# A hybrid decoder layer on one core: key norms as two float32r products of split squares, compressed tokens with 129 columns, pinned orders of pair 4 and of the last pair of a group, and a two-operation scaling

## The chip, the cores and the metric

The kernel is one program on one core of a Trainium2 chip. TensorE (PE) does the matrix products and transposes, VectorE (DVE), ScalarE (ACT) and GpSimd (POOL) the work on elements, and SyncE (SP) and ACT issue most transfers. The metric is the device time of one execution in microseconds (us): lower is better.

## The reference

One decoder layer for 512 tokens of width 1024, in float32. What the change touches, cut from the reference:

```python
kk = heads(k * k_k)                                            # RWKV-7 half, 16 heads of 64
kk = kk / jnp.maximum(jnp.sqrt(jnp.sum(kk * kk, axis=-1, keepdims=True)), 1e-12)
...
cidx = np.arange(n_cmp)[:, None] * CMP_STRIDE + np.arange(CMP_BLOCK)[None, :]   # 31 blocks of 32 tokens, stride 16
def compress(t, pos, w1, w2):                                  # sparse attention half, 4 groups of keys and values
    blk = kv(t)[:, :, cidx] + pos.astype(f32)
    hid = jax.nn.gelu(blk.reshape(B, G, n_cmp, CMP_BLOCK * DH) @ w1.astype(f32))
    return hid @ w2.astype(f32)
...
e = jnp.where(mask, jnp.exp(s - jnp.max(s, axis=axis, keepdims=True)), 0.0)     # masked softmax
return e / jnp.maximum(jnp.sum(e, axis=axis, keepdims=True), TINY)
```

The layer normalises its input, projects it, runs RWKV-7 time mixing (16 heads) and sparse attention (compressed, selected and window branches, 16 heads) beside each other, merges them by gates, and ends with a gated feed-forward block.

## The kernel before, in words

**Products.** A large product with float32 inputs is done as three products of type float32r: each factor is split into a high part (a copy rounded to float32r) and a low part (the rest), and high by high, high by low and low by high are summed. `proj_steps` (L302 to L309) does one block of a projection so: 8 steps, each of three products 128x512 (L306, L307, L308), with a yield after each step. A step is called a group below, a group of three products. Its weights come in two halves; each half is loaded by a transfer that SP issues, copied to the high part by ACT (L124, called from `split_to`), and subtracted to the low part by POOL (L162). Each of these has three buffers, so the copy of a later half waits until PE has finished with an earlier one. Smaller products are left in float32; the trace records a float32 product as two PE instructions.

**Order.** Python generators lay out the work. `inputs` (L493) projects K, R and V of a pair of heads, `prep` (L526) makes decay, gates and key norms of the pair, `couple` (L581) makes the products between keys and queries within chunks of 64 tokens, `invert` (L644) inverts the chunks' triangles on DVE, `recur` (L688) runs the recurrence, and `finish` (L829) closes a group. The eight pairs form two groups of GP = 4: pairs 0 to 3 and 4 to 7. `drive` (L453) steps the projections and gives the other generators a step at fixed rates; a yield marks where one may be left for another. A scheduler then fixes the order of instructions on each engine. Each engine runs its list in that order. `keep_in_program_order` pins an instruction's place among its engine's others.

**Shifts.** A projection's result is mixed with its own shift by one token: `shift_a` on ACT (L333) and `shift_b` on DVE (L336), both reading the projection's bank of PSUM. `shift_b` of K is pinned at step SK = 4 of the projection of R. Two banks (`pj`) are used in turn by the projections of K, R, V and the others.

**Key norms.** `prep` squares the scaled keys (Q, L531, ACT), multiplies them by a matrix of ones (`onesr`, in float32, L548), which sums within each head and spreads the sums over its rows (pb); DVE bounds pb below (L549), ACT takes Ln (L555) and Exp (L556), and DVE uses it in KB (L567) and AR (L570). The gates (pw L533, pa L541) stand ahead of it; POOL's T (L538) lies between pw and the scan (L539). Tiles of the tag "T" (Q, C, T, F, EN and others) share NT = 6 buffers.

**couple.** After two yields PE transposes V (pv, L140) and multiplies KB by AR (g, L605, two banks of `pz` and two of `py`); after more yields it transposes KB (pt) and does pl and pbo.

**invert.** The inversion of a group is a chain of small DVE instructions (TM L660, XP L662), 30 steps, beside which the next projections run. Group 0's chain runs while pair 4's K and R are projected.

**Compression.** `cproj` (L384) projects the tokens to be compressed into KC, with one array of 33 columns for each of four groups and a fifth for the positions; `compress` (L405) multiplies 16 slices of it by w1 in float32 (hid, L412: 155 columns, five times 31), and yields after every fourth.

**Attention.** `score` (L1051) makes the probabilities of a pair of heads; `norm` (L1063) divides them: for each piece of 128 queries and 128 to 512 keys one `tensor_scalar` by a column of reciprocals on DVE and one on POOL (both L1073). The pieces are then transposed on PE (pt, L140).

Of the kernel before, what the change touches and what calls it, by code (L numbers as in the profile page):

```python
# [10 lines left out]
F32 = mybir.dt.float32  # L11
F32R = mybir.dt.float32r
AF = mybir.ActivationFunctionType
OP = mybir.AluOpType
# [28 lines left out]
def hybrid_layer(ctx: ExitStack, tc: tile.TileContext, a, out, dbg=None, stop=None):  # L43
# [33 lines left out]
    def pz(name):  # L77
        return pzs[-1][1].tile([128, 512], F32, tag="pz", name=name, bufs=2)
# [253 lines left out]
    def shift_a(p, o, mc, n=128):  # L332
        sc.activation(o, p[:n], AF.Copy, scale=omm[:n, mc:mc + 1])  # L333
# [50 lines left out]
    def cproj(kv):  # L384
        KC = cp.tile([128, 5, 8, 33], F32, tag="KC", name=f"KC{kv}", bufs=2)
        KCs.append(KC)
        po.memset(KC[:, 4], 0.0)
        pos = cp.tile([64, 32], F32, tag="pos", name=f"pos{kv}", bufs=2)
        sy.dma_start(pos, a["posk" if kv == 0 else "posv"])
        po.memset(KC[:, 0:4, :, 32:33], 0.0)  # L390
        for i in range(2):
            po.tensor_copy(KC[64 * i:64 * i + 64, 4, :, 0:2].rearrange("p r q -> p q r"),
                           pos.rearrange("p (q r two) -> p q r two", r=8, two=2)[:, :, :, i])
        for half in range(2):
# [6 lines left out]
            for e in range(2):  # L401
                for i in range(2):
                    sc.dma_start(KC[64 * i:64 * i + 64, 2 * half + e, :, 0:32], z[e * 64:e * 64 + 64, i])

    def compress(kv):  # L405
# [5 lines left out]
        for l in range(16):  # L411
            te.matmul(ph[:, 0:5 * NCMP], w1[:, l, :], KCs[kv][:, :, l % 8, l // 8:l // 8 + NCMP],  # L412
                      start=l == 0, stop=l == 15)
            if l % 4 == 3:
                yield
        hb = cp.tile([128, 1], F32, tag="hb", name=f"hb{kv}", bufs=2)
        ve.tensor_copy(hb, ph[:, 4 * NCMP:4 * NCMP + 1])
        u = cp.tile([128, 4, 32], F32, tag="hu", name=f"hu{kv}", bufs=2)
        w = cp.tile([128, 4, 32], F32, tag="hv", name=f"hv{kv}", bufs=2)
        po.memset(u, 0.0)  # L420
        ve.tensor_scalar(u[:, :, 0:NCMP], ph[:, 0:4 * NCMP].rearrange("p (g n) -> p g n", n=NCMP), hb, None,
                         op0=OP.add)
# [70 lines left out]
    def inputs(p, o):  # L493
        K = o.K = rw.tile([128, S], F32, tag="K", name=f"K{p}", bufs=2)
        pk = pj(f"k{p}")
        yield from proj_steps(4 + 3 * p, f"k{p}", pk)
        shift_a(pk, K, 8 + p)
        R = o.R = rw.tile([128, S], F32, tag="R", name=f"R{p}", bufs=1)
        pr = pj(f"r{p}")
        for i, _ in enumerate(proj_steps(3 + 3 * p, f"r{p}", pr)):  # L500
            if i == SK:
                tc.keep_in_program_order(shift_b(pk, K, 8 + p))
            yield
# [22 lines left out]
    def prep(p, o, gr=None):  # L526
        K, R, VW, lh, ll = o.K, o.R, o.VW, o.lh, o.ll
        V = VW[:, 64:]
        kkc = vec[:, V_KK + p:V_KK + p + 1]
        Q = rw.tile([128, S], F32, tag="T", name=f"Q{p}", bufs=NT)  # L530
        sc.activation(Q, K, AF.Square, scale=kkc)  # L531
        pw = pz(f"pw{p}")
        te.matmul(pw, lh[:, :128], ltw, start=True, stop=False)  # L533
# [10 lines left out]
        F = rw.tile([128, S], F32, tag="T", name=f"F{p}", bufs=NT)  # L544
        sc.activation(F, pa, AF.Identity, scale=hka[:, p:p + 1], bias=oka[:, p:p + 1])
        yield
        pb = pz(f"pb{p}")
        te.matmul(pb, onesr.bitcast(F32), Q, start=True, stop=True)  # L548
        ve.tensor_scalar(pb, pb, 1e-24, None, op0=OP.max)  # L549
# [31 lines left out]
    def couple(p, o, gr, i):  # L581
# [6 lines left out]
        sc.activation(gr.Dc[:, i], EC[:, :, 64], AF.Copy)  # L588
        yield
        yield  # L590
        for q in range(2):
# [459 lines left out]
    def score(p8, o):  # L1051
# [11 lines left out]
        def norm(e, qb, k):  # L1063
# [7 lines left out]
            for b in range(2):  # L1071
                i = b * 4 + k
                (po if b else ve).tensor_scalar(o.pe[e, b, k], o.pe[e, b, k], st[e][:, 3, i:i + 1], None, op0=OP.mult)  # L1073

# [514 lines left out]
```

## Time and profile before

| | us |
|---|---|
| median of 3 runs | 1169.26 (1168.82 to 1169.72) |
| profiled execution, its own time | 1168.92 |
| its span in the trace | 1167.1 |
| busy: PE | 1145.0 |
| busy: DVE, ACT, POOL | 587.8, 584.0, 580.5 |

The granted TensorE clock has a mean of 0.997. The span runs from the first to the last instruction; 1.8 us of the execution's own time lie outside it. In the rows of the profile "L" is the line in the kernel, then come engine, operation and tile, written from left to right as result and inputs. A row of the timeline begins with start and duration in us; what stands in brackets is how long the engine was idle before it, and what it waited for. Matmuls are pipelined: a product's duration (0.39 us) is longer than the distance to the next one's start, and it is this distance that counts.

### The profile page before, as it was taken

The numbers are of one execution on the slowest core, as the hardware profiler recorded it, in microseconds if no ns is written. First come the engines' busy times: TensorE is split into PE (matmuls) and PEld (weight loads), VectorE is DVE, ScalarE is ACT, GpSimd is POOL, SyncE is SP. The second block draws the span as 40 slices with busy tenths as digits, with TensorE's granted clock in tenths as the row PEclk, the third lists the DMA queues.
The fourth block names the chain that finished last, engine by engine and source line by source line (L and its number), as shares of the span: only waits on it lengthen the run. The fifth ranks groups of instructions, "written<-read, shape, count | busy, mean of one in ns | idle before, by whom it ended". The sixth has DMA issues, their size and how long they took to land.

```text
span 1167.1 us, 19728 instructions
## 1 busy us (share of the span) xinstructions
PE 1145.0 (98%) x7338; PEld 916.2 (79%) x7338; DVE 587.8 (50%) x1194; ACT 584.0 (50%) x1150; POOL 580.5 (50%) x526
## 2 busy tenths in 40 slices
PE   9999999999999999989999999999999999999997
PEld 7888878777887887656677778889888888888886
DVE  4226666534676642677798745754443343331103
ACT  5537664453666434567676654434444444443311
POOL 4335654425655443477766635511565566554440
PEclk9999999999999999999999999999999999999999
DMA  6433235321433664115552136641233333334421
GB/s 235 126 83 80 84 105 166 111 86 44 133 113 103 190 182 128 56 42 149 168 156 89 46 98 182 211 153 37 83 99 99 95 95 100 99 94 134 135 64 72
DMA packets 95507, 131.95 MB, mean 113 GB/s; under 512 B 34033, under 2 KB 36913, under 8 KB 95154
## 3 DMA queue, kind: packets, MB, share of 16 engines
q1 hardware_dynamic: 79490, 116.26, 33.3%
q10 hardware_dynamic: 15920, 14.42, 4.0%
q8 instruction: 58, 0.95, 0.3%
q14 instruction: 39, 0.32, 0.1%
HBM read 108.30 MB, written 19.14 MB: 109 GB/s over the span
## 4 chain that ended last, share of the span: by engine, by line
PE 91%; DVE 4%; ACT 2%; POOL 2%; issue 1%; DVEq 0%; POOLq 0%; ACTq 0%
PE pu L221 6%; PE pu L223 6%; PE pu L222 6%; PE dn L1321 3%; PE dn L1320 3%; PE dn L1319 3%; PE o L1146 3%; PE pt L140 3%; PE ub L1203 3%; PE gt L306 2%; PE ub L1205 2%; PE ub L1204 2%; PE gt L307 2%; PE gt L308 2%; PE v L306 2%; PE v L307 2%
## 5 line engine op out<-in xcount | busy, mean ns | idle before, releaser
L1099 ACT ACTIVATE p<-p,stt 128x384 f32<-128x384 f32 (+3 forms) x128 | 70.7, 554 | 35.1 <-DVE stt L1097 33.4
L1073 POOL TENSOR_SCALAR p<-p,stt 128x512 f32<-128x512 f32 (+1 forms) x64 | 72.9, 1149 | 30.7 <-DVE stt L1068 16.4
L1461 DVE SCALAR_TENSOR_TENSOR u<-pu,cvec,u 128x511 f32<-128x511 f32 x44 | 33.0, 749 | 101.1 <-ACT u L1460 101.1
L1097 DVE CUSTOM_DVE_ANT_0 p<-s,rh 128x384 f32<-128x384 f32 (+3 forms) x128 | 59.2, 485 | 24.6 <-PE s L1083 18.9
L140 PE MATMUL pt<-ident,p 128*128 128x128 f32 x320 | 44.7, 274 | 2.9 <-POOL p L1073 2.0
L1467 DVE TENSOR_TENSOR al<-u,ah 128x512 fp32r<-128x512 f32 x22 | 23.9, 1085 | 45.5 <-ACT ah L1466 45.5
L140 PEld LDWEIGHTS pt<-ident,p 128*128 128x128 f32 x320 | 37.9, 141 | 7.8 <-POOL p L1073 2.5
L1146 PE MATMUL o<-PT,vt 128*64 128x384 f32 (+3 forms) x256 | 43.9, 448 | 0.0
L1465 POOL TENSOR_TENSOR u<-u,u 128x512 f32<-128x512 f32 x22 | 28.4, 1290 | 27.2 <-DVE u L1462 26.3
L1090 PE MATMUL s<-kst,qs 128*128 128x512 f32 (+1 forms) x128 | 38.5, 390 | 2.6 <-DVE stt L1097 2.4
L1460 ACT ACTIVATE u<-pu,cvec 128x512 f32<-128x512 f32 x44 | 33.6, 765 | 3.0 <-PE pu L1423 3.0
L1462 DVE SCALAR_TENSOR_TENSOR u<-pu,cvec,u 128x510 f32<-128x510 f32 x44 | 33.0, 749 | 1.6
L1073 DVE TENSOR_SCALAR p<-p,stt 128x512 f32<-128x512 f32 (+1 forms) x64 | 33.2, 548 | 0.8
L1137 ACT ACTIVATE PT<-pt 128x512 f32<-128x512 f32 x48 | 27.6, 586 | 9.2 <-PE pt L140 8.8
L1146 PEld LDWEIGHTS o<-PT,vt 128*64 128x64 f32 x256 | 16.8, 136 | 19.4 <-issue 17.5
L1090 PEld LDWEIGHTS s<-kst,qs 128*128 128x128 f32 x128 | 21.4, 189 | 10.7 <-DVE stt L1097 6.2
L1367 DVE TENSOR_TENSOR p2ss<-p2ss 128x1 f32<-128x1 f32 x4 | 0.6, 161 | 52.1 <-ACT p2jl L1365 52.1
L1139 DVE COPY PT<-pt 128x512 f32<-128x512 f32 x32 | 21.6, 676 | 8.3 <-PE pt L140 8.3
L1466 ACT ACTIVATE ah<-u 128x512 fp32r<-128x512 f32 x22 | 13.9, 633 | 22.1 <-POOL u L1465 22.1
L1099 ACT ACTIVATION_READ_ACCUMULATOR p<-p,stt 128x1 f32 x128 | 24.1, 189 | 0.0
L809 ACT ACTIVATE UV<-xs 64x256 f32<-64x256 f32 x16 | 6.0, 378 | 35.0 <-PE xs L804 34.6
L662 DVE TENSOR_TENSOR XP<-XP,TM 128x30 f32<-128x30 f32 (+14 forms) x60 | 20.3, 338 | 2.0
(1758 smaller groups left out, 3939.4 us busy)
## 6 DMA issues: line engine op xcount, KB each, us to landing
gtd<-gt ACTq DMA_DIRECT2D x16, 256.0 KB, 2.8
qs<-qd SPq DMA_DIRECT2D x32, 128.0 KB, 3.3
g<-gtd SPq DMA_DIRECT2D x16, 256.0 KB, 3.0
xt<-in_x_dram SPq DMA_DIRECT2D x4, 512.0 KB, 5.2
bvd<-bv SPq DMA_DIRECT2D x8, 256.0 KB, 2.3
bvl<-bvd SPq DMA_DIRECT2D x8, 256.0 KB, 2.9
kst<-kst ACTq DMA_DIRECT2D x16, 128.0 KB, 2.3
t<-oad SPq DMA_DIRECT2D x8, 256.0 KB, 3.3
```

What stands on the lines that cost most here:

```text
L140: return te.transpose(o, i, ident)
L221: te.matmul(p, wh(k), mh(k), start=first and k == 0, stop=False)
L222: te.matmul(p, wh(k), ml(k), start=False, stop=False)
L223: te.matmul(p, wl(k), mh(k), start=False, stop=last and k == n - 1)
L306: te.matmul(p, wh(k), hh[:, k, :], start=k == 0, stop=False)
L307: te.matmul(p, wh(k), hl[:, k, :], start=False, stop=False)
L1073: (po if b else ve).tensor_scalar(o.pe[e, b, k], o.pe[e, b, k], st[e][:, 3, i:i + 1], None, op0=OP.mult)
L1090: m = te.matmul(s_[:, :n], qt, kt[:, x, b, :n], start=x == 0, stop=x == 1)
L1097: ve.tensor_tensor_reduce(sb, parts[b], rh[e][:, (3 - qb) * 128:], -1.0, BIG, OP.add, OP.min, st[e][:, 0, i:i + 1])
L1099: sc.activation(sb, sb, AF.Exp, scale=-1.0, bias=st[e][:, 0, i:i + 1], accum_out=st[e][:, 1, i:i + 1])
L1146: te.matmul(acc[e * 64:e * 64 + 64, j * 128:], vt[:, j, b * 256 + g * 64:b * 256 + g * 64 + 64], m[e][:, c:c + n], start=False, stop=k == ...
L1203: te.matmul(p, wh(k), sh[:, k, :], start=k == 0, stop=False)
```

## The change

1. **Compressed tokens.** KC becomes one array with the position columns first (0 and 1) and the four groups behind them with 32 columns each. A slice for a product is then 129 neighbouring columns instead of five pieces of 31. Four POOL memsets go. The 16 products of a kind stand in two runs of eight instead of four of four.
2. **Key norms.** Q is split into Qh (ACT copy) and Ql (POOL subtraction), and pb is the sum of two float32r products with `onesr`. They are written directly behind the gate products, before the yield. That is 8 more ACT copies, 8 more POOL subtractions, and two more tiles of tag "T" for each pair.
3. **Pair 4.** `shift_b` of its K is written directly behind `shift_a`, and no longer pinned at step 4 of R.
4. **couple.** The last pair of each group (3 and 7) yields three times, not twice, ahead of the transposes and the products g.
5. **Scaling.** POOL's `tensor_scalar` in `norm` gets a second operation, a multiplication by 1.0; the one on DVE stays.

```diff
--- before.py
+++ after.py
@@ -382,14 +382,12 @@
     KCs = []
 
     def cproj(kv):
-        KC = cp.tile([128, 5, 8, 33], F32, tag="KC", name=f"KC{kv}", bufs=2)
+        KC = cp.tile([128, 8, 130], F32, tag="KC", name=f"KC{kv}", bufs=2)
         KCs.append(KC)
-        po.memset(KC[:, 4], 0.0)
         pos = cp.tile([64, 32], F32, tag="pos", name=f"pos{kv}", bufs=2)
         sy.dma_start(pos, a["posk" if kv == 0 else "posv"])
-        po.memset(KC[:, 0:4, :, 32:33], 0.0)
         for i in range(2):
-            po.tensor_copy(KC[64 * i:64 * i + 64, 4, :, 0:2].rearrange("p r q -> p q r"),
+            po.tensor_copy(KC[64 * i:64 * i + 64, :, 0:2].rearrange("p r q -> p q r"),
                            pos.rearrange("p (q r two) -> p q r two", r=8, two=2)[:, :, :, i])
         for half in range(2):
             p = pj(f"kc{kv}{half}")
@@ -400,7 +398,8 @@
                 sc.activation(z[:, i], pv[:, i], AF.Copy)
             for e in range(2):
                 for i in range(2):
-                    sc.dma_start(KC[64 * i:64 * i + 64, 2 * half + e, :, 0:32], z[e * 64:e * 64 + 64, i])
+                    c = 2 + 32 * (2 * half + e)
+                    sc.dma_start(KC[64 * i:64 * i + 64, :, c:c + 32], z[e * 64:e * 64 + 64, i])
 
     def compress(kv):
         w1 = cp.tile([128, 16, 128], F32, tag="w1", name=f"w1{kv}", bufs=2)
@@ -409,16 +408,16 @@
         sy.dma_start(w2, a["w2k" if kv == 0 else "w2v"])
         ph = pz(f"hid{kv}")
         for l in range(16):
-            te.matmul(ph[:, 0:5 * NCMP], w1[:, l, :], KCs[kv][:, :, l % 8, l // 8:l // 8 + NCMP],
-                      start=l == 0, stop=l == 15)
-            if l % 4 == 3:
+            te.matmul(ph[:, 0:129], w1[:, l, :], KCs[kv][:, l % 8, l // 8:l // 8 + 129], start=l == 0, stop=l == 15)
+            if l % 8 == 7:
+                yield
                 yield
         hb = cp.tile([128, 1], F32, tag="hb", name=f"hb{kv}", bufs=2)
-        ve.tensor_copy(hb, ph[:, 4 * NCMP:4 * NCMP + 1])
+        ve.tensor_copy(hb, ph[:, 0:1])
         u = cp.tile([128, 4, 32], F32, tag="hu", name=f"hu{kv}", bufs=2)
         w = cp.tile([128, 4, 32], F32, tag="hv", name=f"hv{kv}", bufs=2)
         po.memset(u, 0.0)
-        ve.tensor_scalar(u[:, :, 0:NCMP], ph[:, 0:4 * NCMP].rearrange("p (g n) -> p g n", n=NCMP), hb, None,
+        ve.tensor_scalar(u[:, :, 0:NCMP], ph[:, 2:130].rearrange("p (g n) -> p g n", n=32)[:, :, 0:NCMP], hb, None,
                          op0=OP.add)
         ve.tensor_tensor(w, u, u, op=OP.mult)
         ve.tensor_scalar(w, w, 0.044715, 1.0, op0=OP.mult, op1=OP.add)
@@ -495,10 +494,12 @@
         pk = pj(f"k{p}")
         yield from proj_steps(4 + 3 * p, f"k{p}", pk)
         shift_a(pk, K, 8 + p)
+        if p == GP:
+            shift_b(pk, K, 8 + p)
         R = o.R = rw.tile([128, S], F32, tag="R", name=f"R{p}", bufs=1)
         pr = pj(f"r{p}")
         for i, _ in enumerate(proj_steps(3 + 3 * p, f"r{p}", pr)):
-            if i == SK:
+            if i == SK and p != GP:
                 tc.keep_in_program_order(shift_b(pk, K, 8 + p))
             yield
         shift(pr, R, p)
@@ -528,7 +529,11 @@
         V = VW[:, 64:]
         kkc = vec[:, V_KK + p:V_KK + p + 1]
         Q = rw.tile([128, S], F32, tag="T", name=f"Q{p}", bufs=NT)
+        Ql = rw.tile([128, S], F32R, tag="T", name=f"Ql{p}", bufs=NT)
+        Qh = rw.tile([128, S], F32R, tag="T", name=f"Qh{p}", bufs=NT)
         sc.activation(Q, K, AF.Square, scale=kkc)
+        sc.activation(Qh, Q, AF.Copy)
+        po.tensor_tensor(Ql, Q, Qh.bitcast(F32), op=OP.subtract)
         pw = pz(f"pw{p}")
         te.matmul(pw, lh[:, :128], ltw, start=True, stop=False)
         te.matmul(pw, ll[:, :128], ltw, start=False, stop=True)
@@ -543,9 +548,10 @@
         sc.activation(pa, pa, AF.Tanh, scale=0.5, bias=ha0[:, p:p + 1])
         F = rw.tile([128, S], F32, tag="T", name=f"F{p}", bufs=NT)
         sc.activation(F, pa, AF.Identity, scale=hka[:, p:p + 1], bias=oka[:, p:p + 1])
-        yield
         pb = pz(f"pb{p}")
-        te.matmul(pb, onesr.bitcast(F32), Q, start=True, stop=True)
+        te.matmul(pb, onesr, Qh, start=True, stop=False)
+        te.matmul(pb, onesr, Ql, start=False, stop=True)
+        yield
         ve.tensor_scalar(pb, pb, 1e-24, None, op0=OP.max)
         EC = rw.tile([128, 8, 65], F32, tag="EC", name=f"EC{p}", bufs=1)
         EN = rw.tile([128, S], F32, tag="T", name=f"EN{p}", bufs=NT)
@@ -586,8 +592,8 @@
             sc.activation(AR[:, 0, :], Q, AF.Copy)
         po.tensor_tensor(AR[:, 1, :].rearrange(c8, t=64), R.rearrange(c8, t=64), EC[:, :, 1:65], op=OP.mult)
         sc.activation(gr.Dc[:, i], EC[:, :, 64], AF.Copy)
-        yield
-        yield
+        for _ in range(3 if i == GP - 1 else 2):
+            yield
         for q in range(2):
             pv = px(f"pv{p}{q}")
             for j in range(4):
@@ -1070,7 +1076,11 @@
                                  op=OP.mult)
             for b in range(2):
                 i = b * 4 + k
-                (po if b else ve).tensor_scalar(o.pe[e, b, k], o.pe[e, b, k], st[e][:, 3, i:i + 1], None, op0=OP.mult)
+                w = st[e][:, 3, i:i + 1]
+                if b:
+                    po.tensor_scalar(o.pe[e, b, k], o.pe[e, b, k], w, 1.0, op0=OP.mult, op1=OP.mult)
+                else:
+                    ve.tensor_scalar(o.pe[e, b, k], o.pe[e, b, k], w, None, op0=OP.mult)
 
         done = []
         for e, qb in ((0, 3), (0, 2), (1, 3), (1, 2), (0, 1), (0, 0), (1, 1), (1, 0)):
```

How this moves the instructions, at three places. On PE, where pair 1's key norms stand in the projection of pair 2's K; before:

```order
L308 MATMUL k_1119<-hh,k2l_1121 128x512
L306 MATMUL k_1119<-hh,k2h_1120 128x512
L307 MATMUL k_1119<-hl,k2h_1120 128x512
L548 MATMUL pb_1157<-Q_1135,onesr 128x512
L308 MATMUL k_1119<-hh,k2l_1121 128x512
L306 MATMUL k_1119<-hh,k2h_1126 128x512
```

and after:

```order
L308 MATMUL k_1120<-hh,k2l_1122 128x512
L306 MATMUL k_1120<-hh,k2h_1121 128x512
L307 MATMUL k_1120<-hl,k2h_1121 128x512
L552 MATMUL pb_1156<-Qh_1138,onesr 128x512
L553 MATMUL pb_1156<-Ql_1137,onesr 128x512
L308 MATMUL k_1120<-hh,k2l_1122 128x512
L306 MATMUL k_1120<-hh,k2h_1127 128x512
```

The two products Qh and Ql stand at the same place as the one of Q, between the second and the third product of the same group. It is the same in pairs 1, 2, 3, 5, 6 and 7; in pair 0 they stand four products earlier than before, in pair 4 about ten. On POOL, Ql stands directly ahead of the next R weights' low part and of T in each pair.

On PE, behind the products g of pair 3, in the block gt10 (a gate projection) and the next one, gt01; before:

```order
L605 MATMUL g_1745<-AR_860,KB_1665 128x128
L605 MATMUL g_1746<-AR_860,KB_1665 128x128
L306 MATMUL gt_1690<-hh,gt10h_1697 128x512
L307 MATMUL gt_1690<-hl,gt10h_1697 128x512
L308 MATMUL gt_1690<-hh,gt10l_1698 128x512
L306 MATMUL gt_1690<-hh,gt10h_1697 128x512
L307 MATMUL gt_1690<-hl,gt10h_1697 128x512
L308 MATMUL gt_1690<-hh,gt10l_1698 128x512
L306 MATMUL gt_1690<-hh,gt10h_1697 128x512
L307 MATMUL gt_1690<-hl,gt10h_1697 128x512
L308 MATMUL gt_1690<-hh,gt10l_1698 128x512
L306 MATMUL gt_1773<-hh,gt01h_1774 128x512
```

and after:

```order
L611 MATMUL g_1767<-AR_856,KB_1681 128x128
L611 MATMUL g_1768<-AR_856,KB_1681 128x128
L306 MATMUL gt_1706<-hh,gt10h_1713 128x512
L307 MATMUL gt_1706<-hl,gt10h_1713 128x512
L308 MATMUL gt_1706<-hh,gt10l_1714 128x512
L306 MATMUL gt_1786<-hh,gt01h_1787 128x512
```

Three groups of gt10 stood behind pair 3's g, now one does: the transposes pv and the products g have moved behind two groups (six products) that stood behind them. Pair 7 is alike.

On DVE, in the inversion chain of group 0, where the shifts of pair 4's R and K stand (V is the one after them); before:

```order
L662 TENSOR_TENSOR XP_1878<-XP_1878,TM_1850 128x4x27
L336 SCALAR_TENSOR_TENSOR R_2084<-r_2085,vec,R_2084 128x511
L660 TENSOR_TENSOR TM_1850<-XL_1849,XP_1878 128x84
L662 TENSOR_TENSOR XP_1878<-XP_1878,TM_1850 128x3x28
L660 TENSOR_TENSOR TM_1850<-XL_1849,XP_1878 128x58
L662 TENSOR_TENSOR XP_1878<-XP_1878,TM_1850 128x2x29
L660 TENSOR_TENSOR TM_1850<-XL_1849,XP_1878 128x30
L662 TENSOR_TENSOR XP_1878<-XP_1878,TM_1850 128x30
L336 SCALAR_TENSOR_TENSOR K_2042<-k_2043,vec,K_2042 128x511
L336 SCALAR_TENSOR_TENSOR V_2125<-v_2127,vec,V_2125 128x511
```

and after:

```order
L668 TENSOR_TENSOR XP_1894<-XP_1894,TM_1866 128x13x18
L666 TENSOR_TENSOR TM_1866<-XL_1865,XP_1894 128x228
L336 SCALAR_TENSOR_TENSOR K_2058<-k_2059,vec,K_2058 128x511
L668 TENSOR_TENSOR XP_1894<-XP_1894,TM_1866 128x12x19
L666 TENSOR_TENSOR TM_1866<-XL_1865,XP_1894 128x220
L668 TENSOR_TENSOR XP_1894<-XP_1894,TM_1866 128x11x20
```

The shift of K has moved from behind the last step of the chain into it, ahead of the XP step 12x19, nine steps earlier than the shift of R stood; R's own shift now stands behind the step 7x24. With this the bank of PSUM that pair 4's V takes has changed too: before, it was the bank of R, which DVE frees by the shift of R; now it is the bank of K, which DVE frees by the shift of K.

More of the change, by code (lines that the diff above doesn't have):

```diff
@@ L545, in prep @@
         sc.activation(F, pa, AF.Identity, scale=hka[:, p:p + 1], bias=oka[:, p:p + 1])
+        pb = pz(f"pb{p}")
+        te.matmul(pb, onesr, Qh, start=True, stop=False)
+        te.matmul(pb, onesr, Ql, start=False, stop=True)
         yield
-        pb = pz(f"pb{p}")
-        te.matmul(pb, onesr.bitcast(F32), Q, start=True, stop=True)
         ve.tensor_scalar(pb, pb, 1e-24, None, op0=OP.max)
```

## The prediction

> **What bounds the kernel now.** I read the page for busy times and the chain that ended last, then the waits of PE, then PE's timeline around each edit, and last the other engines at those places.
>
> ```profile
> PE 1145.0 (98%) x7338; PEld 916.2 (79%) x7338; DVE 587.8 (50%) x1194; ACT 584.0 (50%) x1150; POOL 580.5 (50%) x526
> ...
> PE 91%; DVE 4%; ACT 2%; POOL 2%; issue 1%; DVEq 0%; POOLq 0%; ACTq 0%
> ```
> ```profile
> PE pct L140 <- POOL sc L1049: 2.2, 1, 2.2
> PE pt L140 <- POOL p L1073: 2.0, 2, 1.3
> PE v L306 <- DVE R L336: 2.0, 1, 2.0
> PE g L605 <- DVE AR L570: 1.9, 2, 0.9
> ```
>
> PE is busy for 98% and is 91% of the chain. An edit gains only if it shortens PE's own work or ends one of its waits; the other engines are half idle, and what is added there costs only where PE comes to wait for it. The second fence gives, for each kind of wait, its sum in us, how often, and the longest; these four kinds lie where the change reaches, 8.1 us together.
>
> The measure for a product moved or saved is the distance from one float32r product to the next:
>
> ```profile
> 205.13 0.39 PE L308 MATMUL r<-hh,r4l 128*128 128x512 f32 x1
> ...
> 207.17 0.39 PE L308 MATMUL r<-hh,r4l 128*128 128x512 f32 x1
> 209.55 0.50 PE L306 MATMUL v<-hh,v4h 128*128 128x512 f32 x1 [1.98 <-DVE R L336]
> ```
>
> Nine steps lie between the first two rows: 2.04 / 9 = 0.227 us each.
>
> **Key norms.** Pair 1, on PE:
>
> ```profile
> 110.14 1.02 PE L548 MATMUL pb<-Q,onesr 128*128 128x512 f32 x2
> ...
> 111.23 0.40 PE L306 MATMUL k<-hh,k2h 128*128 128x512 f32 x1
> ...
> 117.39 1.03 PE L140 MATMUL pv<-ident,V 128*128 128x128 f32 x8
> 118.57 0.90 PE L605 MATMUL g<-AR,KB 64*128 64x128 f32 x11
> ```
>
> From pb to L306 are 1.09 us, of which one product (L308) is 0.227: pb costs 0.86. Two float32r products cost 0.454. So 0.41 are saved in each of eight pairs, 3.3 in all, if PE doesn't wait behind. Whether it does is seen at g, which needs AR from DVE:
>
> ```profile
> 110.38 0.63 ACT L124 ACTIVATE r2h<-r21r 128x512 fp32r<-128x512 f32 x1 [1.07 <-POOL T L538]
> ...
> 116.52 0.58 ACT L556 ACTIVATE pb<-pb 128x512 f32<-128x512 f32 x1
> ```
> ```profile
> 117.75 0.68 DVE L570 SCALAR_TENSOR_TENSOR AR<-Q,pb 128x512 f32<-128x512 f32 x1
> ```
> ```profile
> 93.54 1.03 PE L140 MATMUL pv<-ident,V 128*128 128x128 f32 x8
> 94.50 1.72 PE L605 MATMUL g<-AR,KB 64*128 64x128 f32 x26
> ...
> 317.88 1.03 PE L140 MATMUL pv<-ident,V 128*128 128x128 f32 x8
> 318.84 0.60 PE L605 MATMUL g<-AR,KB 64*128 64x128 f32 x6
> ...
> 344.56 1.03 PE L140 MATMUL pv<-ident,V 128*128 128x128 f32 x8
> 345.73 0.72 PE L605 MATMUL g<-AR,KB 64*128 64x128 f32 x8
> ```
>
> In pairs 0 and 5 g starts 0.96 after pv: no wait. In pair 1 it is 1.18 and in pair 6 1.17, so PE already waits 0.2 there, though the waits list no such row; AR ended at 118.43, g began at 118.57. That AR comes at the end of a chain on ACT (r2h at 110.38, then F, EC, EN, Ln, a table load, Exp at 116.52) that is as long as before. It starts with r2h, whose buffer PE frees by products ahead of pb (POOL's T, named in the row, had ended earlier), so a shorter pb doesn't bring AR forward. I take no gain in pairs 1, 2 and 6, and 0.41 in pairs 0, 4 and 5: 1.2. Both ends stay in the range (0 to 3.3).
>
> The cover of Qh and Ql:
>
> ```profile
> 106.76 0.63 ACT L124 ACTIVATE r2h<-r20r 128x512 fp32r<-128x512 f32 x1 [2.00 <-issue]
> ```
> ```profile
> 107.47 1.30 POOL L162 TENSOR_TENSOR r2l<-r20r,r2h 128x512 fp32r<-128x512 f32 x1 [2.37 <-ACT r2h L124]
> ```
>
> ACT is idle for 2.00 behind Q, and a copy takes about 0.6; POOL is idle for 2.37 ahead of this subtraction, and a subtraction takes 1.30. Both fit, so I cost them at nothing. Without that cover T, behind them on POOL, and with it scan, AR and g would be up to 1.3 late in each pair.
>
> **couple.** Pair 3:
>
> ```profile
> 165.96 1.03 PE L140 MATMUL pv<-ident,V 128*128 128x128 f32 x8
> 167.95 1.05 PE L605 MATMUL g<-AR,KB 64*128 64x128 f32 x14 [0.95 <-DVE AR L570]
> ```
>
> Here g comes 1.99 behind pv, 1.03 more than unhindered; pair 7 is the other of the two such waits in the list. With pb 0.41 shorter and AR as before, 1.44 would be missing. The six products that now come first take 6 x 0.227 = 1.36, so 0.08 stays. Gain: 2 x (1.44 - 0.08) = 2.7. Group 0's inversion begins some 0.3 later for it; the next paragraph shows its slack.
>
> **Pair 4.** V's first product should have come at 207.40 and came at 209.55: 2.15 lost, for the bank that DVE frees by the shift of R.
>
> ```profile
> 202.52 0.67 ACT L333 ACTIVATE K<-k,vd 128x512 f32<-128x512 f32 x1
> ```
> ```profile
> 208.74 0.75 DVE L336 SCALAR_TENSOR_TENSOR R<-r,vec,R 128x511 f32<-128x511 f32 x1 [4.56 <-ACT R L333]
> ...
> 210.80 0.74 DVE L336 SCALAR_TENSOR_TENSOR K<-k,vec,K 128x511 f32<-128x511 f32 x1
> ...
> 216.43 0.75 DVE L336 SCALAR_TENSOR_TENSOR V<-v,vec,V 128x511 f32<-128x511 f32 x1 [4.89 <-ACT V L333]
> ```
>
> After the change V needs K's bank, free once ACT's K (ended 203.19) and a shift of 0.75 are done, at about 204: 3.4 ahead of need. So the whole 2.15 go. The price: K now stands inside the inversion chain, DVE waits there for ACT's K, and the rest of the chain and V's shift are queued behind. That wait replaces the 4.56 that DVE sat ahead of R at about the same depth of the chain's time, so the chain, which ended ahead of K at 210.80, ends later by K's own 0.75 and the 0.3 of pair 3, at about 211.9. V's shift, 2.15 sooner, comes at 214.3: 2.4 of its idle 4.89 are left, and PE sees none of it.
>
> **Compressed tokens.**
>
> ```profile
> L140 PE MATMUL pt<-ident,p 128*128 128x128 f32 x320 | 44.7, 274 | 2.9 <-POOL p L1073 2.0 <-DVE p L1073 0.6 <-DVE PT L1139 0.3
> ...
> L412 PE MATMUL hid<-KC,w 128*128 128x155 f32 x64 | 10.0, 299 | 0.0
> ```
> ```profile
> 56.82 1.24 PE L412 MATMUL hid<-KC,w 128*128 128x155 f32 x8
> ```
>
> Eight hid instructions take 1.24 with a last one of 0.299: (1.24 - 0.299) / 7 = 0.134 each at 155 columns. The pv transposes above, of the same form with 128 columns, take (1.03 - 0.274) / 7 = 0.108. By columns 129 would cost 0.112, by the transposes 0.109: 64 x 0.022 to 0.025 = 1.4 to 1.6. I take 1.5; if the distance doesn't follow the columns it is 0. The memsets leave a POOL that nothing waits for there: 0.
>
> The Trainium skill (TensorE: Matmul & The Clock Gate, section Back-to-back issue gap) gives about 81 ns for a product of 128 columns in a stream of weight loads and products; by it this edit would gain 64 x (0.134 - 0.081) = 3.4. The trace has 0.108 for such a stream here, so that figure stays out of the sum.
>
> **Scaling.**
>
> ```profile
> L1073 POOL TENSOR_SCALAR p<-p,stt 128x512 f32<-128x512 f32 x16 | 27.1, 1691 | 18.7 <-DVE stt L1068 12.1 <-ACT p L1099 6.5
> ...
> L1059 POOL TENSOR_SCALAR rh<-dist 128x512 f32<-128x512 f32 x16 | 10.1, 630 | 5.3 <-DVE stt L1097 4.0 <-PE y L760 0.5
> ...
> L1073 POOL TENSOR_SCALAR p<-p,stt 128x128 f32<-128x128 f32 x16 | 9.7, 605 | 0.0
> ```
> ```profile
> 521.60 0.63 PE L140 MATMUL pct<-ident,sc 128*64 128x128 f32 x4 [2.19 <-POOL sc L1049]
> ```
> ```profile
> 496.88 2.95 POOL L1073 TENSOR_SCALAR p<-p,stt 128x512 f32<-128x512 f32 x2
> ...
> 515.96 3.00 POOL L1073 TENSOR_SCALAR p<-p,stt 128x512 f32<-128x512 f32 x2 [5.01 <-DVE stt L1068]
> 518.94 0.73 POOL L1041 TENSOR_TENSOR sc<-sc,cmask 128x256 f32<-128x256 f32 x1
> ```
>
> One operation with a scalar from a column takes 1691 ns at 512 columns and 605 at 128, 2.83 ns a column; two operations with constants (L1059) take 630 at 512. No row has two operations with a column. It lies between nothing gained and 1.06 gained for each large one. I take the fast end: what L1059 shows is a form with two operations, as the new one is. Then two in a row take 1.3 instead of 3: the two waits of pt for p (2.0 in the list) go, and sc, queued behind such a pair on POOL, comes 1.7 sooner, which leaves 0.5 of 2.19. Sum 2.0 + 1.7 = 3.7; 4.5 if small waits that the list misses go too.
>
> **The sum.** Key norms 1.2, couple 2.7, pair 4 2.15, compressed tokens 1.5, scaling 3.7: 11.25. The profiled execution took 1168.92 of its own, 1157.7 after; the median of the runs is 0.3 above it, so 1158.0. From 0.2%, 2.3 us, a measurement of this kernel can tell a difference.
>
> **The rivals.**
>
> *The column is what makes the scaling slow.* POOL would read the scalar in a slow loop with one operation or two, and the 3.7 stay lost: 1161.7. For it: L1059 and L1073 differ in this as well. Against it: DVE's half of the same line takes a column without such a price, but that is another engine. Chance 0.25. The Trainium skill (GPSIMD Engine Reference, section Elementwise — side-by-side cycle accounting) says that up to two operations POOL's ports set the pace, at 1.03 cycles an element, so that one or two cost the same; by that rule too the edit brings nothing. The 2.83 ns a column of the one-operation row are far above that pace, so the rule doesn't hold for this form as it stands.
>
> *Pair 4's wait stays.* If K's shift is held in the inversion chain until past 207, V waits for it as it did for R: 2.15 given back, 1160.2. Against it: ACT's K ends at 203.19. Chance 0.07.
>
> *Slower: each operation is a pass.* If POOL walks the columns once for each operation, a large one takes 1.69 more. At three places (the two waits of pt for p and the one for sc) PE already waits behind two of them, so all of it goes through: 3 x 2 x 1.69 = 10.1, against 7.55 from the other parts: 1168.92 + 2.6 + 0.3 = 1171.8. It turns the sign from 7.55 / 6 = 1.26 more for each. L1059, with two operations in 630 ns, speaks against it. Chance 0.03.
>
> **How the numbers follow.** The forecast has 0.62, the rivals 0.25, 0.07 and 0.03; 0.03 are left for no change, if two waits of the kind come back elsewhere. Faster 0.94, same 0.03, slower 0.03. The range: down to 1155.5, with the pb gain in three more pairs (1.2), 0.8 more from scaling and 0.5 from hid; up to 1163.5, the first rival with most of pair 4's wait.
>
> **What would show it.** In the profile after: pb as two records 0.227 apart; hid at 0.11; g 0.96 behind pv in pairs 0, 3, 4, 5 and 7, and 1.6 in 1, 2 and 6; no wait of v on R; POOL's L1073 at about 630 ns for 512 columns and no wait of pt on it. It is wrong if L1073 keeps 1691 ns, if g waits in pairs 0 or 5 for a T that Ql made late, or if v waits for K.

## The result, and the profile after

The changed kernel takes 1159.8 us (median of 4 runs, 1158.28 to 1160.91); the kernel before, on the same chip, 1169.04 (4 runs, 1168.27 to 1169.72). The ratio is 0.992, with a 95% interval of 0.9903 to 0.9937: faster by 9.2 us. The forecast was 1158.0, in a range of 1155.5 to 1163.5. The profiled execution took 1158.86 of its own, its span is 1157.1: 10.0 less than the span before.

The page, and the waits of PE after the change:

```profile
PE 1136.9 (98%) x7338; PEld 912.6 (79%) x7338; DVE 585.2 (51%) x1194; ACT 588.2 (51%) x1158; POOL 555.8 (48%) x530
```
```profile
PE g L611 <- DVE AR L576: 1.8, 3, 0.6
...
PE pct L140 <- POOL sc L1055: 0.8, 1, 0.8
PE gt L308 <- POOL gt05l L162: 0.7, 1, 0.7
PE pg L887 <- DVE stt L1107: 0.7, 1, 0.7
PE gt L308 <- POOL gt17l L162: 0.6, 1, 0.6
...
PE pct L140 <- DVE stt L1074: 0.6, 1, 0.6
PE kcm L441 <- DVE hu L427: 0.4, 1, 0.4
```

The wait of V for R and those of pt for POOL's p are gone; g's waits are three of 0.6 instead of two of 0.95. What is new are waits on low parts of weights (gt05l, gt17l), on stt, and at kcm; one of 0.8 in the program's first 10 us is among the rows left out. PE's busy time fell by 8.1.

Where the time came from is read by the start of the same block's first product in both traces (us from the span's start):

| first product of | before | after | gained so far | in this stretch |
|---|---|---|---|---|
| k0 (pair 0's K) | 56.14 | 54.47 | 1.67 | 1.67: the start of the program |
| v0 | 77.31 | 74.46 | 2.85 | 1.18: compressed tokens |
| v1 | 98.66 | 95.55 | 3.11 | 0.26: norms, pair 0 |
| v3 | 147.11 | 143.71 | 3.40 | 0.29: norms, pairs 1 and 2 |
| gt11 | 180.20 | 175.19 | 5.01 | 1.61: pair 3, norms and third yield |
| k4 | 196.52 | 192.56 | 3.96 | -1.05: inversion of group 0 begins |
| v4 | 209.55 | 203.44 | 6.11 | 2.15: V's wait |
| gt14 | 236.85 | 230.29 | 6.56 | 0.45: norms, pair 4 |
| v5 | 298.98 | 293.73 | 5.25 | -1.31: block gt05, mostly |
| v6 | 324.40 | 318.79 | 5.61 | 0.36: norms, pair 5 |
| v7 | 350.00 | 344.31 | 5.69 | 0.08: norms, pair 6 |
| gt17 | 388.48 | 381.23 | 7.25 | 1.56: pair 7 |
| kwp0 | 399.36 | 393.39 | 5.97 | -1.28: inversion of group 1 begins |
| ub (weights wb01) | 615.60 | 605.50 | 10.10 | 4.13: attention, scaling |

The prediction's terms are all there, about 12.1 together; 3.6 are given back at three places that it didn't name, and 1.7 come from the start, which the change doesn't touch. PE's timeline after, at the norms, at g of pairs 1 and 3, and at pair 4's V:

```profile
107.02 0.39 PE L552 MATMUL pb<-Qh,onesr 128*128 128x512 f32 x1
107.25 0.39 PE L553 MATMUL pb<-Ql,onesr 128*128 128x512 f32 x1
107.47 0.39 PE L308 MATMUL k<-hh,k2l 128*128 128x512 f32 x1
...
113.82 1.03 PE L140 MATMUL pv<-ident,V 128*128 128x128 f32 x8
115.46 2.06 PE L611 MATMUL g<-AR,KB 64*128 64x128 f32 x32 [0.60 <-DVE AR L576]
...
163.35 1.03 PE L140 MATMUL pv<-ident,V 128*128 128x128 f32 x8
164.32 2.06 PE L611 MATMUL g<-AR,KB 64*128 64x128 f32 x32
...
203.22 0.39 PE L308 MATMUL r<-hh,r4l 128*128 128x512 f32 x1
203.44 0.39 PE L306 MATMUL v<-hh,v4h 128*128 128x512 f32 x1
```

The pair of products takes 107.47 - 107.02 = 0.45 instead of 0.86. In pair 1, g comes 1.64 behind pv (1.18 before): the 0.41 are lost there. In pair 3 it is 0.97 (1.99 before), unhindered. V follows R without a gap.

The start is a matter of PE's clock. Rows of before, then of after:

```profile
5.28 3.78 PE L119 MATMUL gb<-g1r 1*128 1x512 f32 x4
```
```profile
5.30 1.99 PE L119 MATMUL gb<-g1r 1*128 1x512 f32 x4
```

The same four instructions take 3.78 in one and 1.99 in the other. Of the twelve profiled executions in this study, seven have the long row and five the short one, and the first product of kc00 stands at 33.5 to 34.0 in the seven and at 32.0 to 32.2 in the five. Which it is doesn't follow the edits, and the runs of the changed kernel alone fall into two groups (1158.3 and 1158.9, 1160.7 and 1160.9), so I take it to vary from one execution to the next. It moved the profiled comparison by 1.7. So the experiments below are compared by the **rest**, the span from that product to the end: 1133.2 before (1167.1 - 33.91) and 1124.9 after (1157.1 - 32.21). By the rest the change is worth 8.3.

### The profile page after: what moved, and what is told of

Same layout as the page of the kernel before. It is cut to its first block, busy times and chain, and to the rows that moved or that the text cites. A ratio compares the mean times of both kernels' runs of the same rounds, so it can differ in the third digit from the quotient of the medians.

```text
span 1157.1 us, 19755 instructions
## 1 busy us (share of the span) xinstructions
PE 1136.9 (98%) x7338; PEld 912.6 (79%) x7338; DVE 585.2 (51%) x1194; ACT 588.2 (51%) x1158; POOL 555.8 (48%) x530
## 4 chain that ended last, share of the span: by engine, by line
PE 52%; DVE 1%; POOL 1%; issue 0%; ACT 0%; DVEq 0%; POOLq 0%; ACTq 0%
PE pu L222 6%; PE pu L223 6%; PE pu L221 6%; PE dn L1330 3%; PE dn L1329 3%; PE dn L1331 3%; PE o L1156 3%; PE ub L1213 3%; PE ub L1214 2%; PE ub L1215 2%; PE pt L140 2%; PE s L1100 1%; PE wo L1403 1%; PE wo L1401 1%; PE wo L1402 1%; PE s L1093 1%
## 5 line engine op out<-in xcount | busy, mean ns | idle before, releaser
L1081 POOL TENSOR_SCALAR p<-p,stt 128x512 f32<-128x512 f32 (+1 forms) x64 | 38.8, 617 | 38.6 <-DVE stt L1074 25.3
```

The source lines that it names most:

```text
L1081: po.tensor_scalar(o.pe[e, b, k], o.pe[e, b, k], w, 1.0, op0=OP.mult, op1=OP.mult)
```

## The experiments

My theory after the result: each part brings about what the sum said, and the missing 3.6 go to ACT, where the change has moved copies of weights behind long copies of the inversion. The rival: the parts bring less or more than said, and the losses are transfers that land late.

| kernel | median of runs | ratio to before, 95% | rest |
|---|---|---|---|
| before | 1169.0 | | 1133.2 |
| changed | 1159.8 | 0.9903 to 0.9937 | 1124.9 |
| before, scaling alone | 1163.2 | 0.9949 to 0.9973 | 1129.1 |
| changed, two yields | 1160.5 | 0.9919 to 0.9943 | 1125.2 |
| changed, pair 4 pinned | 1163.0 | 0.9948 to 0.9972 | 1128.7 |
| changed, XP on DVE | 1157.9 | 0.9898 to 0.9923 | 1123.2 |
| changed, one float32 pb | 1162.3 | 0.9925 to 0.9950 | 1126.6 |
| changed, 155 columns | 1160.2 | 0.9917 to 0.9942 | 1126.0 |
| XP on DVE, TT on POOL | 1158.6 | 0.9892 to 0.9925 | 1122.9 |
| the same, third yield but in 0, 4 | 1156.5 | 0.9886 to 0.9919 | 1122.8 |
| the same, third yield but in 0, 4, 5 | 1157.2 | 0.9890 to 0.9923 | 1121.9 |
| changed, rh by one operation | 1169.9 (one run) | | 1134.5 |

Each rest is that of one profiled execution. Each ratio is to the kernel before as it ran beside the row on the same chip, where its median was 1167.7 to 1169.0; medians of different rows can come from different chips. By the ratios only the scaling alone and pair 4 pinned stand clear of the changed kernel; the other differences between variants are read from the block starts of single executions.

**Scaling alone.** In the kernel before:

```diff
-                (po if b else ve).tensor_scalar(o.pe[e, b, k], o.pe[e, b, k], st[e][:, 3, i:i + 1], None, op0=OP.mult)
+                w = st[e][:, 3, i:i + 1]
+                if b:
+                    po.tensor_scalar(o.pe[e, b, k], o.pe[e, b, k], w, 1.0, op0=OP.mult, op1=OP.mult)
+                else:
+                    ve.tensor_scalar(o.pe[e, b, k], o.pe[e, b, k], w, None, op0=OP.mult)
```

> The kernel before with the two-operation scaling alone. If the second operation is what makes POOL's scaling fast, its 128x512 takes about 0.81 us as in the changed kernel (1.69 before), the two waits of pt for p (2.0) go and the wait of pct for sc falls from 2.2 to about 0.8, so 3.0 to 4.0 us less: about 1165.5. If the gain of the changed kernel in the attention stage came from its earlier parts standing otherwise to each other, the scaling gets as short but less than 1.5 us come of it: 1167.5 or more.

Measured: 4.1 less by the rest, 5.6 by the medians. The scaling on POOL in this kernel:

```profile
L1075 POOL TENSOR_SCALAR p<-p,stt 128x512 f32<-128x512 f32 x16 | 12.9, 805 | 22.8 <-DVE stt L1068 20.4 <-ACT p L1103 2.3
...
L1075 POOL TENSOR_SCALAR p<-p,stt 128x128 f32<-128x128 f32 x16 | 5.9, 371 | 0.0
```

A large one takes 0.81 instead of 1.69. So the part stands by itself. But the waits that it ends are smaller than 4.1: pt's 2.0 go and sc's 2.2 become 0.8, while pct now waits 0.6 and pg 0.7 for DVE's stt, 2.1 in all. Another part lies in the clock of the profiled execution of the kernel before (stretches of it: columns are the busy time of the engines, then the granted clock of PE, the share of the DMA engines, GB/s):

```profile
519.40:521.60 2.20, 0.01 (x2) 0.01 (x1) 1.73 (x7) 1.87 (x6) 0.95 (x3) 1.00 0.00 0
522.90:526.30 3.40, 3.40 (x8) 1.36 (x7) 1.50 (x6) 1.98 (x6) 3.31 (x4) 0.50 0.22 36
```

Behind the wait of 2.2, in which PE stood still, the clock was 0.50 for 3.4 us. From pct's start to q5's first product it takes 8.99 there (521.60 to 530.59) and 7.61 with the scaling (516.96 to 524.57): 1.4 lost to the clock. In this kernel's execution and in the changed one's, with a wait of 0.8 there, the clock stays at 1.00. That this is the scaling's doing isn't shown: in the next kernel, which has the fast scaling too, it falls at this place. A last 0.4 comes behind a wait of s for stt (0.2 at 613.15 before), which is gone.

**Two yields.** In the changed kernel:

```diff
-        for _ in range(3 if i == GP - 1 else 2):
-            yield
+        yield
+        yield
```

> The changed kernel with two yields in couple for all pairs (the third yield undone). If the third yield is worth what the prediction gave it, 2.7 us, this is 2.7 slower than the changed kernel: 1162.5, with waits of 1.4 at g in pairs 3 and 7. If most of it is given back in the changed kernel, because the copy XP of the inversion has come to stand on ACT between a gate's eviction and the copy of the next weights, those waits at g come back too, but PE's gaps of about 1.05 at gt02 and 1.3 at ksp0 behind the two inversions' starts go: only 0.2 to 0.6 slower, about 1160.2.

Measured: 0.3 slower by the rest, 0.7 by the medians. At ksp0, behind both inversions' starts, this kernel stands 0.2 ahead of the changed one (387.75 against 387.95); 0.5 are lost later, up to q5, where the clock of this execution was 0.51 on average from 510.2 to 513.6, behind a wait of 1.3 of pg for stt that the changed kernel has as well. The waits at g are back, and the two losses at the inversions' starts are gone. PE's g in pairs 3 and 7, then ACT where the inversion of group 0 begins:

```profile
164.10 2.06 PE L611 MATMUL g<-AR,KB 64*128 64x128 f32 x32 [1.04 <-DVE AR L576]
...
364.62 2.06 PE L611 MATMUL g<-AR,KB 64*128 64x128 f32 x32 [1.04 <-DVE AR L576]
```
```profile
181.97 0.60 ACT L477 ACTIVATE gt<-gt 128x512 f32<-128x512 f32 x1 [2.69 <-PE gt L308]
182.46 0.62 ACT L124 ACTIVATE gt02h<-gt021r 128x512 fp32r<-128x512 f32 x1
```

Against it the same place in the changed kernel, on ACT and on PE:

```profile
180.83 0.60 ACT L477 ACTIVATE gt<-gt 128x512 f32<-128x512 f32 x1 [4.50 <-PE gt L308]
181.96 1.03 ACT L661 ACTIVATE XP<-XL 128x1024 f32<-128x1024 f32 x1 [0.53 <-ACT gt L477]
182.93 0.61 ACT L124 ACTIVATE gt02h<-gt021r 128x512 fp32r<-128x512 f32 x1
```
```profile
183.12 0.39 PE L308 MATMUL gt<-hh,gt02l 128*128 128x512 f32 x1
183.59 0.50 PE L306 MATMUL gt<-hh,gt02h 128*128 128x512 f32 x1
...
184.95 0.50 PE L308 MATMUL gt<-hh,gt02l 128*128 128x512 f32 x1 [0.34 <-POOL gt02l L162]
```

With three yields XP, the first copy of the inversion, stands on ACT between a gate's eviction (gt, L477) and the copy of gt02's second half. That copy then starts 2.1 behind the eviction's start instead of 0.5, and PE, which needs it at 183.35 and its low part from POOL after that, loses 1.05. ksp0 in group 1 is alike (1.28). So the third yield gains 2.1 at g (2.3 by the block starts) and loses 2.3 here: nothing.

**XP on DVE.** In the changed kernel:

```diff
-        sc.activation(XP.rearrange("u i c -> u c i"), LU, AF.Copy)
+        ve.tensor_copy(XP.rearrange("u i c -> u c i"), LU)
```

> The changed kernel with the inversion's first copy (XP from XL) on DVE instead of ACT. If that copy's place on ACT, ahead of the copy of the second half of the next weights, costs PE the 1.05 at gt02 and the 1.3 at ksp0, both gaps go and the time falls by 1.5 to 2.4: about 1157.7. If the gaps come from transfers that land late (weights, or XL itself), PE waits as before and the time stays within 0.5 of the changed kernel's 1159.8.

Measured: 1.7 less by the rest, 1.9 by the medians. DVE had been idle and makes the copy as soon as XL has landed; on ACT nothing stands between eviction and weights:

```profile
180.53 1.23 DVE L661 COPY XP<-XL 128x1024 f32<-128x1024 f32 x1 [5.20 <-DMA XL<-ld]
```
```profile
182.15 0.60 ACT L477 ACTIVATE gt<-gt 128x512 f32<-128x512 f32 x1 [4.50 <-PE gt L308]
...
183.21 0.63 ACT L124 ACTIVATE gt02h<-gt021r 128x512 fp32r<-128x512 f32 x1 [0.46 <-ACT gt L477]
```

XL had landed at 180.5, 2 us before ACT had done the eviction (182.75). So late transfers were not the cause: the place on ACT was. Up to k4, behind group 0's inversion start, 0.7 of the 1.05 are won back, up to ksp0 1.0 of the 1.28. The copy of gt02's second half still starts 1.06 behind the eviction, not 0.5 as with two yields; why ACT is idle for 0.46 ahead of it stays open.

**Pair 4 pinned.** In the changed kernel:

```diff
-        if p == GP:
-            shift_b(pk, K, 8 + p)
...
-            if i == SK and p != GP:
+            if i == SK:
```

> The changed kernel with pair 4's shift of K pinned at step 4 of R again, as in all other pairs. If that part is worth the wait of V for R's bank, as predicted, the wait (2.0 to 2.2) is back and the time is 2.15 longer: 1162.0. If V's wait was moved elsewhere rather than removed, less than 0.7 is lost: 1160.5 or less.

Measured: 3.8 slower by the rest, 3.2 by the medians: more than either said. On PE, and the stretch behind it (columns as above):

```profile
205.59 0.50 PE L306 MATMUL v<-hh,v4h 128*128 128x512 f32 x1 [1.99 <-DVE R L336]
```
```profile
206.40:209.80 3.40, 3.40 (x9) 2.63 (x8) 2.54 (x10) 0.00 (x0) 0.00 (x0) 0.50 0.30 93
```

The wait is back with the 2.15 that the prediction gave it (203.44 against 205.59), and behind it the clock was halved for 3.4 us, which cost another 1.7. The kernel before had the same wait, without a halved clock behind it in its profiled execution.

**One float32 pb.** In the changed kernel:

```diff
-        Ql = rw.tile([128, S], F32R, tag="T", name=f"Ql{p}", bufs=NT)
-        Qh = rw.tile([128, S], F32R, tag="T", name=f"Qh{p}", bufs=NT)
...
-        sc.activation(Qh, Q, AF.Copy)
-        po.tensor_tensor(Ql, Q, Qh.bitcast(F32), op=OP.subtract)
...
-        te.matmul(pb, onesr, Qh, start=True, stop=False)
-        te.matmul(pb, onesr, Ql, start=False, stop=True)
+        te.matmul(pb, onesr.bitcast(F32), Q, start=True, stop=True)
```

> The changed kernel with pb as one float32 product of Q again, at the new place, without Qh and Ql. The prediction's sum gives the two products 0.41 in pairs 0, 4 and 5 and the same, filled by the third yield, in 3 and 7: about 2.0 slower than the changed kernel, 1161.8. If the shorter pb counts in every pair, 3.3 slower: 1163.1. If the part gives some of its gain back at gt05, where the copies of both halves of the weights have come to stand on ACT behind two copies TT from XL (4.05 us), that wait (0.7 to 0.95) goes here and only 0.8 to 1.3 are lost: 1160.9. In the trace, g's wait of 0.6 in pairs 1, 2 and 6 should fall to about 0.2.

Measured: 1.7 slower by the rest, 2.5 by the medians. The first's number is near, but its account isn't what the blocks show: up to q0 the kernel loses 2.7 at the norms (0.4 each in pairs 0, 4 and 5, 0.6 each in 3 and 7, 0.3 in 1, 2 and 6 together) and makes up 1.3 at gt05, as the third said. Pair 1 in this kernel:

```profile
116.47 1.03 PE L140 MATMUL pv<-ident,V 128*128 128x128 f32 x8
117.65 0.79 PE L606 MATMUL g<-AR,KB 64*128 64x128 f32 x9
```

g is 1.18 behind pv, as in the kernel before, so the shorter pb is what makes it 1.64. And the wait for gt05l, of which the third spoke, is not in this kernel: from gt04's start to k5's, the block behind gt05, it makes up 1.25 on the changed one. The changed kernel's ACT there, with the row on PE:

```profile
234.25 4.05 ACT L724 ACTIVATE TT<-XL 32x1024 f32<-32x1024 f32 x2
238.32 0.63 ACT L124 ACTIVATE gt05h<-gt050r 128x512 fp32r<-128x512 f32 x1
```
```profile
240.42 0.50 PE L308 MATMUL gt<-hh,gt05l 128*128 128x512 f32 x1 [0.68 <-POOL gt05l L162]
```

Before, and with one float32 pb, the copy of gt05's first half stood ahead of the two TT copies. With Qh and Ql in the program it stands behind them.

**155 columns.** In the changed kernel, KC and `compress` as before (part 1 of the diff undone).

> The changed kernel with the compressed tokens as before (five pieces, 155 columns, four groups of four). The prediction gives the 129 columns 1.5 us: 1161.3. The traces of the two kernels show 1.15 by the first products of V of pair 0, with a new wait of 0.4 at kcm: then about 1.1 slower, and the wait at kcm gone. If the columns didn't set the distance between the products, no change.

Measured: 1.1 slower by the rest, 0.4 by the medians, within their spread. The products in the changed kernel:

```profile
L411 PE MATMUL hid<-KC,w 128*128 128x129 f32 x64 | 7.9, 276 | 0.0
```
```profile
58.33 1.95 PE L411 MATMUL hid<-KC,w 128*128 128x129 f32 x16
```

(1.95 - 0.276) / 15 = 0.112 each, 0.0225 less than 0.134: 1.4 for 64. The wait at kcm (0.4) takes a part. It comes from DVE, which makes hu for kcm by a chain of small operations; with the new order one of them runs beside a subtraction of weights on POOL. DVE and POOL in the changed kernel, then the same DVE operation with 155 columns:

```profile
71.17 1.42 DVE L424 TENSOR_TENSOR hv<-hv,hu 128x128 f32<-128x128 f32 x1
```
```profile
71.15 1.29 POOL L162 TENSOR_TENSOR v0l<-v01r,v0h 128x512 fp32r<-128x512 f32 x1 [2.63 <-ACT v0h L124]
```
```profile
74.99 0.29 DVE L425 TENSOR_TENSOR hv<-hv,hu 128x128 f32<-128x128 f32 x1
```

The operation takes 1.42 instead of 0.29 and ends 0.15 behind POOL's. With 155 columns POOL's subtraction has ended before it starts. All nine kernels with 129 columns have both the long operation and the wait of 0.36; the three with 155 have neither.

**XP on DVE, TT on POOL.** On top of XP on DVE:

```diff
-        evict(act_m)
...
-            behind(sc.activation(gr.diag[0][lo, :, 0:32], gr.diag[1][lo], AF.Copy))
+            po.tensor_copy(gr.diag[0][lo, :, 0:32], gr.diag[1][lo])
```

> The changed kernel with the inversion's first copy (XP from XL) on DVE, and the two copies TT from XL on POOL instead of ACT. If those copies ahead of both halves of gt05's weights cost PE about 0.9 at gt05, this is 0.6 to 0.9 faster than the kernel with XP on DVE alone (1157.9), so about 1157.1. If POOL, which then makes them ahead of the low parts of gt04's weights, is late for these instead, PE waits at gt04 and nothing is gained, 1157.9 or more.

Measured: 0.3 less by the rest; the medians can't tell (1158.6 and 1157.9). In group 0 the wait at gt05 is gone and 1.25 gained (gt04's start to k5's); in group 1, 1.1 are lost (q1's start to q2's), since POOL's copies, up to 3.06 each, now stand ahead of q1's low part. So POOL is late, as the second said, but in the other group:

```profile
PE q L308 <- POOL q1l L162: 0.8, 1, 0.8
```

**Third yield in more pairs.** On top of that:

```diff
-        for _ in range(3 if i == GP - 1 else 2):
+        for _ in range(3 if i else 2):
```

> The kernel with XP on DVE and TT on POOL, and a third yield in couple for all pairs but 0 and 4. If AR's chain on ACT is what ate the shorter pb in pairs 1, 2 and 6, six products more ahead of their g cover its waits (0.6 shown, 0.67 by the distance from pv to g, each): the three waits go and the time falls by 1.8 to 2.0, to about 1156.5. If the waits come from a chain that PE's own products start later along with g, or if what stands behind couple (its eviction, transfers, the next V) is late instead, nothing or less than 0.7 is gained.

Measured: 0.1 less by the rest, 2.1 by the medians, which come from two chips; the ratios (0.9908 and 0.9903) can't tell the two apart. In pairs 1, 2 and 6 the waits are gone, and 0.5, 0.4 and 0.5 gained up to the next V. Pair 5, which had no wait, lost 1.1, because its pv was split and waits for a copy on ACT. Pair 1's pv and g on PE, and pair 5's row in the waits of PE:

```profile
115.02 1.03 PE L140 MATMUL pv<-ident,V 128*128 128x128 f32 x8
115.99 2.06 PE L611 MATMUL g<-AR,KB 64*128 64x128 f32 x32
```
```profile
PE pv L140 <- ACT UV L603: 0.7, 1, 0.7
```

**The same with two yields in pair 5** (`3 if i and p != GP + 1 else 2`).

> As the kernel with a third yield for all pairs but 0 and 4, now with two yields in pair 5 as well, where the third one split pv and made PE wait for the eviction of V (0.7 shown, 1.15 by the later blocks). If the gains in pairs 1, 2 and 6 stand by themselves, those 1.15 come on top: about 1155.5. If pair 6's gain hung on pair 5's later place, no change: 1156.5.

Measured: 0.9 less than the last by the rest, 1121.9, the shortest of all. From v5 to v6 the 1.1 come back; 0.3 are lost at r0, where the other kcm now waits for hu, since DVE's operation falls behind POOL's in this chain too (1.43). The medians, 1157.2 and 1156.5, say otherwise, within what the start moves: the profiled execution of this kernel had the long start, that of the last the short one. Both beat the kernel before; against the changed kernel their rests are 3.0 and 2.1 shorter, but the intervals of the ratios overlap.

**One operation with a constant.** In the changed kernel, at L1065:

```diff
-            po.tensor_scalar(rh[e], dist, float(2.0 ** (-8.0 * (h + 1) / 16)), 1.0, op0=OP.mult, op1=OP.mult)
+            po.tensor_scalar(rh[e], dist, float(2.0 ** (-8.0 * (h + 1) / 16)), None, op0=OP.mult)
```

> The changed kernel with rh (L1065, a constant times a tile, 128x512 on POOL, 0.63 us with two operations) by one operation with a constant. If the missing second operation is what made the scaling slow, it takes about 1.7 us like the scaling before. If the scalar from a column was what cost, it stays at 0.63 us. The time itself tells nothing at this size.

```profile
L1065 POOL TENSOR_SCALAR rh<-dist 128x512 f32<-128x512 f32 x16 | 24.5, 1532 | 8.7 <-DVE stt L1107 7.6 <-PE y L766 0.5
```

1532 ns instead of 633 (the changed kernel's mean): the missing second operation is the cost. The column adds the little that is left, 1691 against 1532 with one operation and 809 against 633 with two. This one run took 1169.9. On PE, a transpose (vtp) now waits 4.5 for ACT up to 489 and q5 waits 1.8 instead of 0.9 up to 530, and at each the clock is halved for 6.8 us, from 487.5 and from 531.9.

## Why the prediction was right, and where it was not

- **What a pb and a product cost**: right. 0.45 measured for the two products, 0.454 worked out.
- **Pairs 1, 2 and 6 gain nothing, g comes 1.6 behind pv**: right (1.64, 1.64 and 1.63; 0.4 were gained in the three together). From the start of r2h on ACT to that of AR on DVE the chain takes 7.37 in pair 1, before (110.38 to 117.75) and after (107.27 to 114.64), and with more products ahead of g the waits went and 1.5 were gained: AR's chain had eaten the gain. Pairs 0, 4 and 5 gained 0.26, 0.45 and 0.36, 1.1 for 1.2.
- **"Both fit, so I cost them at nothing"** (Qh and Ql): right at T and AR, where g's gap grew only by the shorter pb. It failed at gt05, where in the program with Qh and Ql a copy of weights stands behind TT: 1.25 by the kernel without them, which has neither this order nor the wait.
- **couple, 2.7**: right at g, where pairs 3 and 7 gained 3.2 with their norms in it, and g came unhindered, without the 0.08 that was to stay. The step that failed is "Group 0's inversion begins some 0.3 later": I asked only when the chain ends, and not what its first instruction, XP, is queued ahead of on ACT. That gave back 2.3.
- **Pair 4, 2.15**: right, to the hundredth, and the chain's delay cost PE nothing. Undone, it cost more in the execution shown, since there the clock fell behind the wait.
- **Compressed tokens, 1.5**: the products gained 1.4, the stretch 1.2, for the wait at kcm, a term that the sum hadn't. The Trainium skill's 81 ns (TensorE: Matmul & The Clock Gate, section Back-to-back issue gap), which would have made 3.4 of it, is not met here: 112 ns at 129 columns.
- **Scaling, 3.7**: 4.1, right by two errors. The waits that the sum named gave about 2.1, because stt on DVE is late next, and a large one takes 0.81, not 0.63; 1.4 are the clock that fell behind a wait of 2.2 in the profiled execution of the kernel before, which is luck as far as the runs show. The first rival, that the column costs, is out: one operation with a constant takes 1.53. The Trainium skill (GPSIMD Engine Reference, section Elementwise — side-by-side cycle accounting), by which one or two operations cost the same, does not hold for this instruction in these runs.
- **The total**: the forecast of 1158.0 was 1.8 below the measured median. Terms of 12.1 less 3.6 given back are 8.4, with 1.7 from the start 10.1; the rest says 8.3. The forecast's 11.25 was too high by what ACT gave back, which the extra at g and the clock made up only in part.

That each of the three losses is ACT's order is shown for two (XP at both inversions, by the kernel with XP on DVE, which won back 1.7 of 2.3) and for gt05 (by the TT copies moved, 1.25). What the last 0.6 of the 2.3 are stays open. Why the scheduler's order differs stays open too: the order was read from the programs, and its cause not tried.

## What to carry to other kernels

Where a step is moved later, look not only at the end of the chain that it starts but at that chain's first instruction on every engine: here a copy of 1 us came to stand ahead of a weight copy, and took back all that a third yield had gained. A gain at one wait is read at the next one; before the change the distance from the transposes to g showed a wait of 0.2 that the list of waits did not. And an execution can differ from the next by more than an edit's worth in its first 15 us, so parts are compared from a common mark on.

## What the runs showed of the hardware

- POOL's `tensor_scalar` with one operation takes 1.53 (a constant) to 1.69 us (a column) at 128x512, with two 0.63 (constants) and 0.81 (a column and a constant).
- A `tensor_tensor` 128x128 on DVE that starts 7 to 14 ns behind one of 128x512 on POOL takes 1.42 to 1.43 us instead of 0.29 (ten cases in nine kernels). Where the two start within 3 ns, it is POOL's that takes longer, 1.45 instead of 1.29 (eight cases).
- Behind a wait of PE the clock can be halved for 3.4 us: behind 2.2 at 521 before, behind 2.0 at 206 with pair 4 pinned, behind 1.3 at 508 with two yields; it cost 1.4, 1.7 and 0.5 more than the wait itself. It doesn't always: the wait of 2.0 at 209 before and that of 1.3 at 508 after had the full clock behind them. The Trainium skill (TensorE: Matmul & The Clock Gate, section What's actually happening) tells of a free-running window of about 3.4 us by which PE's activity is judged; the length of 3.4 and the chance in it agree with these rows. So does the start: in the changed kernel's execution the full clock comes at 5.3 us and is halved again from 8.8 to 12.2, while in that of the kernel before eight transposes that start at 12.52 still take 1.91, where the eight of pv take 1.03.
